# One layer of short convolution and 16-expert mixture: modulation in five groups, and five smaller moves

## Chip, core and metric

One Trainium2 (trn2) chip, one core. The metric is the device time of one execution in microseconds (us). Before the change it is 1913.16 us (median of three runs, 1910.98 to 1913.17). The profile is of one further execution.

## The reference

Everything is float32, with D = 1024 channels and L = 2048 tokens; DEPTH is 1, so the layer is of kind 0 (short convolution).

```python
sh1, sc1, g1, sh2, sc2, g2 = split(silu(c) @ ada_w + ada_b, 6)
hl = rms_norm(x, norm_g[0]) * (1 + sc1) + sh1
b, g, v = split(hl @ sc_w_in, 3)
x1 = x + g1 * ((b * dwconv_centred(g * v, sc_conv)) @ sc_w_out)
h2 = rms_norm(x1, norm_g[1]) * (1 + sc2) + sh2
aff = softmax(h2 @ moe_router)
gate, idx = top_k(aff.T, 256)                     # each of 16 experts picks 256 of 2048 tokens
hid = silu(h2[idx] @ w_gate[e]) * (h2[idx] @ w_up[e])
out = x1 + g2 * scatter_add(gate * (hid @ w_down[e]))
```

## The kernel before

**Precision.** A float32 product is made of three passes: each operand is split into a high part (ACT copies it to fp32r) and a low part (original minus high, by DVE or POOL), and PE adds high*high, high*low and low*high. Weights come in pieces of 512 KB ("raw", loaded on SP's queue), are split into "ws" tiles (8 buffers) and dropped from raw as soon as the low part is made; that releases the next load (`split_high`, `split_low`, `load_to`, lines 199 to 230).

**Stage 1, the in-projection (lines 362 to 625).** The 2048 rows are four quarters of 512. For quarter 0, `load_x` brings four blocks of x, `norm_x` scales each row by its rms (square sum on ACT, power on POOL, product on DVE). Then, for each of 8 k-tiles of 128 channels, `to_hl` turns x by four PE transposes, applies scale A1 and shift sh1 on ACT (twice: high part, and full), and subtracts for the low part. A1 and sh1 are not known at the start: they are columns of `silu(c) @ ada_w`, one pair for each k-tile. `load_ada_cols(k)` brings 1 MB for a k-tile in runs of 128 floats (512 bytes), `ada_cols(k)` adds its 8 row blocks on DVE in two accumulators of 256 columns and then adds the two, `ada_sum(k)` sums over partitions by PE, and `ada_fix(k)` adds bias and gain in three small DVE instructions. The weights of the first two channel tiles (ct 0 and 1; three pieces each, for the three parts of w_in) come in 6 pieces of 128 columns by 1024 rows, the first three in two halves (`load_half`, `split_half`); most of their low parts are made by POOL. The loop at line 544 runs k-tile by k-tile: ct 0 at k, ct 1 with a lag of 3, nine matmuls of 512 columns each (`in_mm`). Behind k = 6 and k = 7 the next quarter's x is normalised and all of its 8 k-tiles are turned. `constants` (line 106) makes tables for the later search, mostly on POOL. Then 30 steps (ps_, ct, q), each 72 matmuls, work off the rest; `in_out` convolves each result and stores it.

**Stage 2, out-projection and router (lines 628 to 940).** 16 blocks of 128 rows.

**Stage 3, experts (lines 943 to 1230).** A short search finds the thresholds of experts 0 and 1; the long one for all 16 (`search_all`, 15 steps, each hit counts on DVE and ACT, a small PE matmul, and an update on DVE) is run in slices: each `tick` runs one slice between matmul groups of experts 0 and 1. `pick_oh(e)` and `pick(e)` turn places into row indices on DVE and PE and gather the expert's rows by two indirect DMAs on POOL. Expert 0's rows are turned by PE (`fetch`), with 6 matmuls on `warm` ahead; the others by a DMA transpose on SP (`turn`) and then put together by DVE and ACT (`join`). `gate_up(e, half)` is 8 k-steps of 24 matmuls of 256 columns, `down(e, half)` 4 steps of 12 matmuls of 512 columns. Both take a function that is called between steps: this is where ticks, picks, turns and joins are placed by hand. The result of an expert is scaled on DVE into `ot` (line 1174) and added into the output by two indirect DMAs of 512 KB on POOL (line 1180).

**Order.** The schedule is manual: each engine works off its instructions in the order in which the program text makes them, and so does each DMA queue (SP's, POOL's). The span ends when the last scatter has landed.

Of the kernel before, what the change touches and what calls it, by code (L numbers as in the profile page):

```python
# [17 lines left out]
P = 128  # L18
# [25 lines left out]
def block_kernel(ctx: ExitStack, tc, x, c, ada_w, ada_b, norm_g, w_in, conv, w_out, router, wg, wu, wd, out):  # L44
# [24 lines left out]
    def row_cols(name, parts):  # L69

        t = consts.tile([P, P], F32, name=name)
        nc.gpsimd.memset(t, 0.0)
        r = 0
        for src, offset, n in parts:
            nc.sync.dma_start(t[r:r + n], dram(src, offset, [[P, n], [1, P]]))
            r += n
        return t, r
# [28 lines left out]
    def constants(scratch):  # L106
# [57 lines left out]
        for t in cnts:  # L164
            nc.vector.tensor_copy(t, zero1)
# [10 lines left out]
    pieces, n_load, n_high, n_done = [], 0, 0, 0  # L176
# [10 lines left out]

    def load_piece(i):
# [7 lines left out]
        nc.sync.dma_start(t, dram(src, offset, ap))  # L196
# [36 lines left out]
    def load_half(i, g):  # L233
        nonlocal n_load
        src, offset, ap, shape = pieces[i]
        if g == 0:
            raws[i] = wpool.tile([P] + shape, F32, name="raw", tag="raw", bufs=n_raw)
            n_load += 1
        n = shape[0] // 2
        nc.sync.dma_start(raws[i][:, g * n:(g + 1) * n],  # L240
                          dram(src, offset + g * n * ap[1][0], [ap[0], [ap[1][0], n], ap[2]]))

    def split_half(i, g, eng=None):
        nonlocal n_high, n_done
        if g == 0:
            ws_of[i] = wpool.tile([P, 2] + pieces[i][3], F32R, name="ws", tag="ws", bufs=n_split)
            n_high += 1
        t, n = ws_of[i], pieces[i][3][0] // 2
        s = slice(g * n, (g + 1) * n)
        nc.scalar.activation(t[:, 0, s], raws[i][:, s], AF.Copy)  # L250
        (eng or nc.vector).tensor_sub(t[:, 1, s], raws[i][:, s], t[:, 0, s].bitcast(F32))
        if g:
            raws.pop(i)
            n_done += 1
            load_to(i + n_raw)

# [105 lines left out]
    with tc.tile_pool(name="mix", bufs=1) as mix:  # L362

        def b4(name):
            return mix.tile([P, D], F32, name=name, tag="b4", bufs=9)
# [21 lines left out]
        def norm_x(q, b, eng=None):  # L387
            t = xq[q][b]
            r = rstd_of(t, junk)
# [5 lines left out]
        def to_hl(q, k, between=lambda: None, eng=None):  # L395
# [127 lines left out]
        for i in range(3):  # L523
            load_half(i, 0)
# [728 lines left out]
```

## Time and profile before

| | |
|---|---|
| median of 3 runs | 1913.16 us |
| the profiled execution | 1912.57 us, of which the span from first to last instruction is 1910.8 us |
| PE busy | 1836.3 us (96%), 11568 matmuls |
| DVE, ACT, POOL busy | 1136.9, 823.7, 304.4 us |
| chain that ended last | PE 89%, DVE 4%, DMA 3% |
| mean granted clock of PE | 0.983 |

PE is busy for nearly all of the span, so time can be had only where PE waits, or where it works at half its clock; the views below look at those stretches: 0 to 87 us, 790 to 837 us, some places up to 960 us, and the last 10 us. Times are from the start of the span.

### The profile page before, as it was taken

The page shows a single profiled execution, that of the slowest core. Times are in us where ns is not written, and L with a number is a line of the kernel's source. Part 1 is how long each engine was busy: PE and PEld are TensorE (multiplying, and loading weights), DVE is VectorE, ACT ScalarE, POOL GpSimd, SP SyncE. Part 2 cuts the span into 40 slices and gives each one's busy share as a digit, 9 for nine tenths or more (in the row PEclk, how much of TensorE's full clock was granted, in tenths as well). Part 3 has the DMA queues.
Part 4 walks back from the last instruction along what each step waited for, and adds up shares of the span by engine and source line. Part 5 has one row for each costly group of instructions (what it writes and reads, how often), then busy time and mean ns, then how long its engine had stood idle before and what let it go on. Part 6 is the DMA issues. An engine that isn't in the chain of part 4 may idle for free.

```text
span 1910.8 us, 29082 instructions
## 1 busy us (share of the span) xinstructions
PE 1836.3 (96%) x11568; PEld 1628.8 (85%) x11568; DVE 1136.9 (60%) x1633; ACT 823.7 (43%) x1046; POOL 304.4 (16%) x457
## 2 busy tenths in 40 slices
PE   4999999999999999579999999999999999999998
PEld 2888888888888888469899999999999999999996
DVE  7654425444325677877766656665765666576653
ACT  3421116211113555547545444554555455445532
POOL 3310002100111122310021102101210211121001
PEclk8999999999999999879999999999999999999999
DMA  9434242344226989466687887779787877878774
GB/s 281 145 113 146 77 160 61 105 137 143 72 72 190 259 257 257 134 219 201 214 249 216 242 248 249 231 227 266 220 239 236 258 219 241 255 238 236 221 231 89
DMA packets 308316, 375.30 MB, mean 196 GB/s; under 512 B 101788, under 2 KB 183764, under 8 KB 308180
## 3 DMA queue, kind: packets, MB, share of 16 engines
q1 hardware_dynamic: 292212, 315.76, 54.3%
q0 software_dynamic: 15968, 57.68, 10.6%
q8 instruction: 91, 1.49, 0.3%
q14 instruction: 45, 0.37, 0.1%
HBM read 300.51 MB, written 50.33 MB: 184 GB/s over the span
## 4 chain that ended last, share of the span: by engine, by line
PE 89%; DVE 4%; DMA 3%; issue 1%; ACT 1%; POOL 1%; SPq 1%; POOLq 0%; DVEq 0%; ACTq 0%
PE pm L1131 12%; PE pm L1133 12%; PE pm L1135 12%; PE pm L451 9%; PE pm L452 9%; PE pm L454 9%; PE pm L1156 6%; PE pm L1154 6%; PE pm L1155 6%; PE pm L656 2%; PE pm L657 2%; PE pm L659 2%; DMA hl<-hl 1%; DMA xt<-in_x_dram 1%; PE pt L398 1%
## 5 line engine op out<-in xcount | busy, mean ns | idle before, releaser
L222 DVE TENSOR_TENSOR ws<-raw,ws 128x1024 fp32r<-128x1024 f32 x434 | 515.6, 1221 | 272.4 <-ACT ws L212 272.4
L212 ACT ACTIVATE ws<-raw 128x1024 fp32r<-128x1024 f32 x437 | 441.3, 1051 | 410.7 <-PE pm L1135 326.9
L1131 PE MATMUL pm<-xT,ws 128*128 128x256 f32 x2048 | 568.8, 278 | 0.0
L1133 PE MATMUL pm<-xT,ws 128*128 128x256 f32 x2048 | 567.1, 277 | 1.0 <-DVE xT L1111 0.9
L1135 PE MATMUL pm<-xT,ws 128*128 128x256 f32 x2048 | 566.8, 277 | 0.0
L1133 PEld LDWEIGHTS pm<-xT,ws 128*128 128x128 f32 x2048 | 385.9, 188 | 2.8 <-DVE xT L1111 1.1
L1131 PEld LDWEIGHTS pm<-xT,ws 128*128 128x128 f32 x2048 | 385.3, 188 | 1.7 <-ACT xT L1110 0.3
L1135 PEld LDWEIGHTS pm<-xT,ws 128*128 128x128 f32 x2048 | 385.2, 188 | 0.0
L451 PE MATMUL pm<-hl,ws 128*128 128x512 f32 x768 | 305.9, 398 | 1.0 <-ACT hl L401 1.0
L452 PE MATMUL pm<-hl,ws 128*128 128x512 f32 x768 | 302.0, 393 | 0.0
L454 PE MATMUL pm<-hl,ws 128*128 128x512 f32 x768 | 217.3, 391 | 0.0
L1180 POOL DMA_INDIRECT out_dram<-ot,idx x32 | 108.0, 3376 | 602.9 <-DVE ot L1174 598.8
L1156 PE MATMUL pm<-ws,hT 128*128 128x512 f32 x512 | 201.6, 394 | 0.0
L1154 PE MATMUL pm<-ws,hT 128*128 128x512 f32 x512 | 201.3, 393 | 0.0
L1155 PE MATMUL pm<-ws,hT 128*128 128x512 f32 x512 | 200.2, 391 | 0.0
L451 PEld LDWEIGHTS pm<-hl,ws 128*128 128x128 f32 x768 | 145.9, 190 | 31.9 <-ACT hl L401 1.4
L452 PEld LDWEIGHTS pm<-hl,ws 128*128 128x128 f32 x768 | 145.9, 190 | 30.5 <-issue 1.0
L454 PEld LDWEIGHTS pm<-hl,ws 128*128 128x128 f32 x768 | 145.5, 189 | 30.8
L461 ACT ACTIVATE cs<-pm 128x512 f32<-128x512 f32 x32 | 19.1, 598 | 332.1 <-issue 261.2
L464 DVE TENSOR_TENSOR u<-cs,pm 128x512 f32<-128x512 f32 x32 | 22.5, 703 | 231.3 <-ACT cs L461 231.3
L1156 PEld LDWEIGHTS pm<-ws,hT 128*128 128x128 f32 x512 | 96.2, 188 | 20.4
L1155 PEld LDWEIGHTS pm<-ws,hT 128*128 128x128 f32 x512 | 96.2, 188 | 20.2
(291 smaller groups left out, 1962.2 us busy)
## 6 DMA issues: line engine op xcount, KB each, us to landing
raw<-in_moe_w_gate_dram SPq DMA_DIRECT2D x128, 512.0 KB, 4.8
raw<-in_moe_w_up_dram SPq DMA_DIRECT2D x128, 512.0 KB, 4.2
raw<-in_moe_w_down_dram SPq DMA_DIRECT2D x128, 512.0 KB, 4.7
raw<-in_sc_w_in_dram SPq DMA_DIRECT2D x45, 512.0 KB, 4.6
xt<-in_x_dram SPq DMA_DIRECT2D x32, 512.0 KB, 7.1
aw<-in_ada_w_dram SPq DMA_DIRECT2D x32, 512.0 KB, 7.1
hl<-in_ada_w_dram SPq DMA_DIRECT2D x32, 256.0 KB, 5.5
hl<-vscr SPq DMA_DIRECT2D x16, 512.0 KB, 4.2
```

Of the source, the lines that this page charges most:

```text
L212: nc.scalar.activation(t[:, 0], raws[n_high], AF.Copy)
L222: (eng or nc.vector).tensor_sub(t[:, 1, ..., s], raw[..., s], t[:, 0, ..., s].bitcast(F32))
L451: nc.tensor.matmul(ps[m], wh, t[:, 0], start=(k == 0), stop=False)
L452: nc.tensor.matmul(ps[m], wl, t[:, 0], start=False, stop=False)
L454: nc.tensor.matmul(ps[m], W(k, m)[0], t[:, 1], start=False, stop=(k == KD - 1))
L1131: nc.tensor.matmul(o, w[:, 0, j, c0], xT[:, 0, k], start=(k == 0 and f % 2 == 0), stop=False, skip_group_check=True)
L1133: nc.tensor.matmul(o, w[:, 0, j, c0], xT[:, 1, k], start=False, stop=False, skip_group_check=True)
L1135: nc.tensor.matmul(o, w[:, 1, j, c0], xT[:, 0, k], start=False, stop=(k == KD - 1), skip_group_check=True)
L1154: nc.tensor.matmul(ps[s], h, w[:, 0, j], start=(k == 0), stop=False)
L1155: nc.tensor.matmul(ps[s], h, w[:, 1, j], start=False, stop=False)
L1156: nc.tensor.matmul(ps[s], l, w[:, 0, j], start=False, stop=(k == KD - 1))
L1180: st = nc.gpsimd.indirect_dma_start(out=out_rows, out_offset=bass.IndirectOffsetOnAxis(ap=idx_of[e][:, s:s + 1], axis=0), in_=ots[s], in_o ...
```

## The change

It does six things. (1) Quarter 0's modulation columns come in five groups, of 1, 1, 2, 2 and 2 k-tiles; groups of two are read in runs of 256 floats (1 KB) and added on DVE in one accumulator of 512 columns. (2) The weights of ct 0 and 1 come together in four steps of 256 rows by 256 columns for each of the three parts, and DVE alone makes their low parts; POOL makes none. `to_hl` is taken apart into `turn_x`, `scale_x` and `low_x`, and quarter 0 is written out with ct 0 and 1 at the same k, with transposes of no use (`wake`) ahead of the first matmul. Five of quarter 1's eight k-tiles are turned within its first step. v_row is loaded on POOL's queue, two of the four row scalings move to ACT, `constants` moves behind the fourth step. (3) The four loads that expert 0's first splits release are issued from POOL's queue, behind the two gathers there; 14, 8 and 3 matmuls of no use stand around its transposes. (4) The search steps of experts 0 and 1 leave out k = 1 and k = 2 behind a stage's begin; the last slice falls behind `down(0, 0)`. (5) Expert 2's turns come one k-step earlier, its joins at k = 7 and at the second step of `down(0, 1)`. (6) The last expert's output goes out in five parts: two left halves behind `down(15, 0)`, then 512, 256 and 256 columns; its last 128 rows are worked off in two lots of 256 columns.

The diff, cut:

```diff
-    def row_cols(name, parts):
+    def row_cols(name, parts, eng=nc.sync):
...
+            eng.dma_start(t[r:r + n], dram(src, offset, [[P, n], [1, P]]))
...
-    pieces, n_load, n_high, n_done = [], 0, 0, 0
+    pieces, n_load, n_high, n_done = [], 6, 6, 6
...
+    load_by = [nc.sync]
...
-        nc.sync.dma_start(t, dram(src, offset, ap))
+        load_by[0].dma_start(t, dram(src, offset, ap))
...
+        if eng:
+            eng.scalar_tensor_tensor(junk, src, 1.0, src, op0=ALU.mult, op1=ALU.mult, accum_out=ss[:, 0:1])
+        else:
+            nc.scalar.activation(junk, src, AF.Square, accum_out=ss[:, 0:1])
...
+        def turn_x(q, k):
+            pt = pt_hl[q, k] = tp.tile([P, QT], F32, name="pt", tag="tp")
             for b in range(4):
                 nc.tensor.transpose(pt[:, b * P:(b + 1) * P], xq[q][b][:, k * P:(k + 1) * P], identf)
...
+        def scale_x(q, k):
+            t = hl[q, k] = hl_tile([P, 2, QT])
             nc.scalar.activation(t[:, 0], pt, AF.Identity, scale=A1[:, k:k + 1], bias=sh1[:, k:k + 1])
             nc.scalar.activation(full, pt, AF.Identity, scale=A1[:, k:k + 1], bias=sh1[:, k:k + 1])
+            return full
+
+        def low_x(q, k, full):
+            nc.vector.tensor_sub(hl[q, k][:, 1], full, hl[q, k][:, 0].bitcast(F32))
+
+        def to_hl(q, k):
+            turn_x(q, k)
+            low_x(q, k, scale_x(q, k))
...
+        groups = [(0, 1), (1, 1), (2, 2), (4, 2), (6, 2)]
+        def load_ada_cols(g):
+            k0, n = groups[g]
+            m = 4 // n
+            ada_t[g] = []
+            for r in range(0, KD, m):
+                t = hl_tile([P, m, 2, n * P], F32)
+                ada_t[g].append(t)
+                for j in range(2):
+                    if n == 1:
+                        nc.sync.dma_start(t[:, :, j], dram(ada_w, r * P * 6 * D + j * D + k0 * P,
+                                                           [[6 * D, P], [6 * D * P, m], [1, P]]))
+                    else:
+                        nc.sync.dma_start(t[:, j], dram(ada_w, (r + j) * P * 6 * D + k0 * P,
+                                                        [[6 * D, P], [D, 2], [1, n * P]]))
...
+        def ada_cols(g, r0=0, r1=KD):
+                ada_a[g] = m2("acc", 2 * n * P)
-                if r < 2:
+                v, t = ada_t[g][r // m][:, r % m].rearrange("p h c -> p (h c)"), ada_a[g]
+                if r == 0:
                     nc.vector.tensor_scalar(t, v, s_col[:, r:r + 1], None, op0=ALU.mult)
                 else:
                     nc.vector.scalar_tensor_tensor(t, v, s_col[:, r:r + 1], t, op0=ALU.mult, op1=ALU.add)
...
+        def ada_sum(g):
...
+        def ada_fix(g, pcol):
+            k0, n = groups[g]
+            s = slice(k0, k0 + n)
+            nc.vector.tensor_add(sh1[:, s], pcol[:, 0], bsh_col[:, s])
+            nc.vector.tensor_add(A1[:, s], pcol[:, 1], bsc_col[:, s])
+            nc.vector.scalar_tensor_tensor(A1[:, s], A1[:, s], 1.0, g0_col[:, s], op0=ALU.add, op1=ALU.mult)
...
         def W_chan(ps_, ct):
+            if ps_ == 0 and ct < 2:
+                return lambda k, m: tuple(w_pair[m, k // 4][:, j, k % 4, ct * P:(ct + 1) * P] for j in range(2))
...
+        def load_w(g):
+            for m in range(3):
+                if g == 0:
+                    w_raw[m, 0] = wpool.tile([P, 4, 2 * P], F32, name="raw", tag="raw", bufs=n_raw)
+                elif g == 2:
+                    w_raw[m, 1] = hl_tile([P, 4, 2 * P], F32) if m else b4("rb", [P, 4, 2 * P])
+                nc.sync.dma_start(w_raw[m, g // 2][:, 2 * (g % 2):2 * (g % 2) + 2],
+                                  dram(w_in, 2 * g * P * 3 * D + m * D, [[3 * D, P], [3 * D * P, 2], [1, 2 * P]]))
...
+        def high_w(g):
+            for m in range(3):
+                if g % 2 == 0:
+                    w_pair[m, g // 2] = wpool.tile([P, 2, 4, 2 * P], F32R, name="ws", tag="ws", bufs=n_split)
+                t, raw, s = part_w(g, m)
+                nc.scalar.activation(t[:, 0, s], raw[:, s], AF.Copy)
...
+        def low_w(g, m):
+            nc.vector.tensor_sub(t[:, 1, s], raw[:, s], t[:, 0, s].bitcast(F32))
...
+        def wake(n):
+            t = mm.tile([P, QT], F32, name="pm", tag="mm")
+            for i in range(n):
+                nc.tensor.transpose(t[:, 0:P], xq[0][0][:, 0:P], identf)
...
+        def mm_pair(i, k):
+            in_mm(pair[i], 0, W_chan(0, i), k)
...
+        load_w(0)
         load_x(0)
+        vrow, nr = row_cols("v_row", [(ada_b, 0, 16), (norm_g, 0, 8), (conv, 0, 24)], nc.gpsimd)
+        for g in range(3):
+            load_ada_cols(g)
+        load_w(1)
+        high_w(0)
+        for m in range(3):
+            low_w(0, m)
+        rs = [rstd_of(xq[0][b], junk) for b in range(4)]
         for b in range(4):
-            norm_x(0, b)
+            norm_x(0, b, nc.scalar if b in (1, 3) else None, rs[b])
         vcols = to_cols("v_col", vrow, nr)
...
+        turn_x(0, 0)
+        wake(14)
+        ada_cols(0)
+        pcol = ada_sum(0)
+        wake(5)
         ada_fix(0, pcol)
+        turn_x(0, 1)
+        full = scale_x(0, 0)
         pair = [new_banks() for _ in range(2)]
+        ada_cols(1, 0, 3)
+        low_x(0, 0, full)
+        ada_cols(1, 3)
+        mm_pair(0, 0)
+        ada_fix(1, ada_sum(1))
+        mm_pair(1, 0)
+        full = scale_x(0, 1)
+        ada_cols(2, 0, 1)
+        low_x(0, 1, full)
+        mm_pair(0, 1)
+        turn_x(0, 2)
+        high_w(1)
+        load_ada_cols(3)
+        load_w(2)
+        ada_cols(2, 1)
+        ada_fix(2, ada_sum(2))
+        for m in range(3):
+            low_w(1, m)
+        load_ada_cols(4)
+        load_w(3)
+        load_x(1)
+        mm_pair(1, 1)
+        turn_x(0, 3)
+        for g in range(2, 5):
+            k = groups[g][0]
+            more_g = g + 1 < len(groups)
+            full = scale_x(0, k)
+            if more_g:
+                ada_cols(g + 1, 0, 2)
+            low_x(0, k, full)
+            mm_pair(0, k)
+            full = scale_x(0, k + 1)
+            if more_g:
+                high_w(g)
+                ada_cols(g + 1, 2, 3)
+            low_x(0, k + 1, full)
+            mm_pair(0, k + 1)
+            if more_g:
+                ada_cols(g + 1, 3)
+                turn_x(0, k + 2)
+            else:
+                rs = [rstd_of(xq[1][b], m2("sq", D, BF), nc.vector) if b % 2 else rstd_of(xq[1][b], junk) for b in range(4)]
                 for b in range(4):
+                    norm_x(1, b, None, rs[b])
                 in_out(pair[0], 0, 0)
+            mm_pair(1, k)
+            if more_g:
+                ada_fix(g + 1, ada_sum(g + 1))
+                for m in range(3):
+                    low_w(g, m)
+            else:
+                to_hl(1, 0)
+            mm_pair(1, k + 1)
+            if more_g:
+                turn_x(0, k + 3)
+        to_hl(1, 1)
+        to_hl(1, 2)
+        load_end[0] = len(pieces)
+        load_to(n_done + n_raw - 1)
...
+            if i == 5:
+                for t in cnts:
+                    nc.vector.tensor_copy(t, zero1.to_broadcast([P, 4]))
...
                 in_mm(ps, q, W_chan(ps_, ct), k)
+                if (ps_, ct, q) == (0, 0, 1) and k + 3 < KD:
+                    to_hl(1, k + 3)
...
+            if i == 3:
+                before, ones_b, tri, slot_r, step, bias, need, zero1, cnts, aux, same, quick = constants(m2)
...
+    def index_parts(parts):
+        for i, (s, c0, n) in enumerate(parts):
+            ix = ix_of[s, c0] = ixs[:, i:i + 1]
+            nc.vector.tensor_scalar(ix, idx_of[E - 1][:, s:s + 1], float(D // n), float(c0 // n), op0=ALU.mult,
+                                    op1=ALU.add)
...
+    def scatter_part(s, c0, n):
+        if parts_of_last:
+            nc.gpsimd.memset(spacer, 0.0)
+        st = nc.gpsimd.indirect_dma_start(
+            out=out.rearrange("b t (c d) -> (b t c) d", d=n), out_offset=bass.IndirectOffsetOnAxis(ap=ix, axis=0),
+            in_=ot_of[E - 1][s][:, c0:c0 + n], in_offset=None, compute_op=ALU.add)
...
+        def finish(s, o, c0, n):
+            nc.vector.scalar_tensor_tensor(ots[s][:, c0:c0 + n], o, gate_of[E - 1][:, s:s + 1], g2b[:, c0:c0 + n],
+                                           op0=ALU.mult, op1=ALU.mult)
+            scatter_part(s, c0, n)
...
+        for k in range(KD):
+            product(0, k)
+        finish(0, ps[0], H, H)
+        for i in range(2):
+            c = slice(i * CAP, (i + 1) * CAP)
+            o = mm.tile([P, CAP], F32, name="pm", tag="mm")
...
+                nc.tensor.matmul(o, h, w[:, 0, j, c], start=(k == 0), stop=False)
+                nc.tensor.matmul(o, h, w[:, 1, j, c], start=False, stop=False)
+                nc.tensor.matmul(o, l, w[:, 0, j, c], start=False, stop=(k == KD - 1))
+            finish(1, o, H + i * CAP, CAP)
...
+            last_down(ps, product)
+            return
...
+        if (e, dh) == (E - 1, 0):
+            index_parts([(0, 0, H), (1, 0, H)])
+            index_parts([(0, H, H), (1, H, CAP), (1, H + CAP, CAP)])
+            for s in range(2):
+                scatter_part(s, 0, H)
...
+    def keep_warm(n):
+        for i in range(n):
+            nc.tensor.matmul(warm, same, ws_of[first][:, 0, 0], start=(i == 0), stop=(i == n - 1))
...
+    keep_warm(14)
+    split_high(first + 4)
+    load_by[0] = nc.gpsimd
     split_to(first + 3)
+    load_by[0] = nc.sync
     for i in (0, 2, 1, 3):
         fetch(0, i, mm)
+        if i > 1:
+            keep_warm(8 if i == 2 else 3)
...
                     (tick(k), turn(1, 0) if k == 7 else None) if k in (2, 4, 5, 6, 7) else None)
             gate_up(0, 1, lambda k: join(1, k // 2 - 2) if k in (4, 6) else
-                    (tick(k), turn(1, 1) if k == 1 else None) if k < 4 else None)
+                    turn(1, 1) if k == 1 else tick(k) if k in (0, 2, 3, 5) else None)
...
-            gate_up(1, 0, lambda k: tick(k) if k else None)
+            gate_up(1, 0, lambda k: tick(k) if k not in (0, 2) else None)
...
-            gate_up(1, 1, lambda k: pick(2) if k == 1 else turn(2, k - 5) if k in (5, 6) else None)
+            gate_up(1, 1, lambda k: pick(2) if k == 1 else turn(2, k - 4) if k in (4, 5) else
+                    join(2, 0) if k == 7 else None)
...
+        down(e - 1, 1, (lambda kk: join(e + 1, 1) if kk == 1 else None) if e + 1 < E else (lambda kk: None))
```

## Rows read from the trace of the kernel before

**Rows 1.** The first stage in one stretch: us, busy us of PE, PEld, DVE, ACT, POOL (instructions), clock, DMA share, GB/s
```profile
0.00:87.00 87.00, 57.12 (x253) 45.40 (x254) 62.29 (x131) 40.93 (x62) 30.23 (x48) 0.90 0.83 234
```
**Rows 2.** What PE waited for, 0 to 130 us: total us, times, longest
```profile
PE pcol L438 <- DVE acc L431: 19.1, 5, 7.0
```
**Rows 3.** DVE (two), POOL (one) by group, 19 to 66 us: busy, mean ns | idle before
```profile
L429 DVE SCALAR_TENSOR_TENSOR acc<-hl,s_col,acc 128x256 f32<-128x256 f32 x42 | 20.7, 550 | 0.1
L431 DVE TENSOR_TENSOR acc<-acc 128x256 f32<-128x256 f32 x7 | 10.5, 1497 | 0.2
...
L222 POOL TENSOR_TENSOR ws<-raw,ws 128x1024 fp32r<-128x1024 f32 x3 | 7.3, 2447 | 9.4 <-ACT ws L212 9.4
```
**Rows 4.** DVE in order of time: start, us, instruction, count
```profile
16.59 0.75 DVE L393 TENSOR_SCALAR xt<-xt,rstd 128x1024 f32<-128x1024 f32 x1 [0.71 <-POOL rstd L283]
...
47.06 0.68 DVE L404 TENSOR_TENSOR hl<-full,hl 128x512 fp32r<-128x512 f32 x1
...
59.79 1.67 DVE L429 SCALAR_TENSOR_TENSOR acc<-hl,s_col,acc 128x256 f32<-128x256 f32 x4
...
75.25 0.75 DVE L469 SCALAR_TENSOR_TENSOR y<-u,v_col,y 128x512 f32<-128x512 f32 x1 [0.85 <-ACT y L468]
76.04 0.75 DVE L471 SCALAR_TENSOR_TENSOR y<-u,v_col,y 128x512 f32<-128x512 f32 x1
...
958.31 2.49 DVE L1053 TENSOR_TENSOR oh<-slot_r,row 128x512 bf16<-128x512 bf16 x4
```
**Rows 5.** Chain that ended last, PE's pieces: start, us
```profile
48.71 0.43 PE pm L452
...
52.44 0.23 PE pm L451
...
59.35 0.50 PE pt L398 x4
```
**Rows 6.** Three stretches, columns as in Rows 1
```profile
45.00:47.00 2.00, 0.46 (x2) 0.01 (x1) 1.97 (x6) 1.45 (x2) 0.00 (x0) 1.00 1.19 291
...
51.00:54.00 3.00, 3.00 (x14) 2.38 (x12) 2.92 (x6) 0.00 (x0) 1.30 (x1) 0.90 1.06 394
...
1907.00:1908.00 1.00, 0.00 (x0) 0.00 (x0) 0.00 (x0) 0.00 (x0) 0.00 (x0) 0.50 1.09 217
```
**Rows 7.** PE in order of time: quarter 1's first matmul, expert 0's start, the last matmul
```profile
86.55 0.39 PE L451 MATMUL pm<-hl,ws 128*128 128x512 f32 x1
...
826.32 1.97 PE L1088 MATMUL pt<-identf,xs 128*128 128x128 f32 x8 [4.10 <-DMA xs<-hscr,idx]
830.77 1.97 PE L1088 MATMUL pt<-identf,xs 128*128 128x128 f32 x8 [2.48 <-DMA xs<-hscr,idx]
832.57 0.58 PE L1131 MATMUL pm<-xT,ws 128*128 128x256 f32 x1
...
1901.56 0.40 PE L1156 MATMUL pm<-ws,hT 128*128 128x512 f32 x1
```
**Rows 8.** POOL in order of time: expert 0's gathers, a scatter of expert 0, the last scatter
```profile
820.70 1.54 POOL L1072 DMA_INDIRECT xs<-hscr,idx  x1 [22.85 <-DVE gate L1077]
822.55 1.80 POOL L1072 DMA_INDIRECT xs<-hscr,idx  x1 [0.30 <-issue]
...
959.73 5.94 POOL L1180 DMA_INDIRECT out_dram<-ot,idx  x1 [0.27 <-issue]
...
1903.02 1.57 POOL L1180 DMA_INDIRECT out_dram<-ot,idx  x1 [3.91 <-DVE ot L1174]
```
**Rows 9.** SP's queue: the first of four loads issued at expert 0's start
```profile
821.29 0.37 SPq L196 DMA_DIRECT2D raw<-in_moe_w_up_dram  x1
```
**Rows 10.** What PE waited for, 130 to 1911 us
```profile
PE pc L965 <- ACT hit L959: 2.5, 2, 1.3
...
PE pm L1133 <- DVE xT L1111: 0.9, 1, 0.9
```

More of the change, by code (lines that the diff above doesn't have):

```diff
@@ L232, in block_kernel @@
     r_of_last = []
[L233 to L255, printed above, removed]
     w_chan = {}
@@ L362, in block_kernel, with b4 @@
     with tc.tile_pool(name="mix", bufs=1) as mix:
[L364 to L365 removed]
+        def b4(name, shape=[P, D]):
+            return mix.tile(shape, F32, name=name, tag="b4", bufs=9)
         def m2(name, n=QT, dt=F32):
@@ L421, in ada_cols @@
+        def ada_cols(g, r0=0, r1=KD):
+            n = groups[g][1]
+            m = 4 // n
             if r0 == 0:
-                ada_a[k] = [m2("acc", 2 * P) for _ in range(2)]
-            acc = ada_a[k]
+                ada_a[g] = m2("acc", 2 * n * P)
             for r in range(r0, r1):
-                v, t = ada_t[k][r // 4][:, r % 4].rearrange("p h c -> p (h c)"), acc[r % 2]
-                if r < 2:
+                v, t = ada_t[g][r // m][:, r % m].rearrange("p h c -> p (h c)"), ada_a[g]
+                if r == 0:
@@ L572, in block_kernel @@
                 for b in range(4):
-                    norm_x(1, b)
-            if k == KD - 1:
+                    norm_x(1, b, None, rs[b])
                 in_out(pair[0], 0, 0)
-            for j in {7: range(2), 8: range(2, 4), 9: range(4, 6), 10: range(6, 8)}.get(k, ()):
-                to_hl(1, j)
-        before, ones_b, tri, slot_r, step, bias, need, zero1, cnts, aux, same, quick = constants(m2)
-        nc.sync.dma_start(rt, dram(router, 0, [[E, P], [E * P, KD], [1, E]]))
-        nc.scalar.activation(rts[:, :, 0], rt, AF.Copy)
@@ L1165, in down @@
         if (e, dh) == (E - 1, 1):
-            for s in range(2):
-                for k in range(KD):
-                    product(s, k)
+            last_down(ps, product)
+            return
         if dh == 0:
@@ L1198, in block_kernel @@
     warm = tp.tile([P, QT], F32, name="warm", tag="tp")
-    for i in range(6):
-        nc.tensor.matmul(warm, same, ws_of[first][:, 0, 0], start=(i == 0), stop=(i == 6 - 1))
+    def keep_warm(n):
[4 more added lines that the diff above has]
+    load_by[0] = nc.gpsimd
     split_to(first + 3)
+    load_by[0] = nc.sync
     for i in (0, 2, 1, 3):
         fetch(0, i, mm)
+        if i > 1:
+            keep_warm(8 if i == 2 else 3)
     for e in range(E):
```

113 lines of the change are left out of this document (30 added, 83 removed).

## The prediction, made blind

> **What bounds the kernel now.** I read the page first: PE is busy 96% of the span, so only places where PE waits or runs at its lower clock can give time. The busy times by stretch say where: in the first 87 us PE is busy 57.12 us [rows 1], and part of that is at half speed, since a matmul of 512 columns takes 0.43 us at 48.71 and 0.23 us at 52.44 [rows 5], which are the 1.2 and 2.4 GHz levels. The waits of PE name the cause: five times, 19.1 us in all, PE waited for the sum of modulation columns on DVE [rows 2]. DVE's groups tell why DVE is late. An accumulation of 256 columns takes 0.42 us undisturbed (four in 1.67 [rows 4]), but 0.55 us in the mean of 42; the closing addition of the same size takes 1.50 us in the mean of seven, while POOL's subtraction takes 2.45 us [rows 3]. DVE loses some 42 x 0.13 + 7 x 1.08 = 13 us to POOL's subtractions. So the stage is bound by DVE, and PE, fed in drops, loses its clock: from 45 to 47 us PE worked 0.46 of 2 us and the granted clock was still 1.00, at 48.71 the pitch is the lower one, and after unbroken work it is the upper one at 52.44 [rows 5, 6]. Quarter 1's first matmul is at 86.55 [rows 7]. After that I read three short places: expert 0's start, where the second gather lets PE go on at 830.77 only [rows 7]; the search, 2.5 us in two waits, and one wait of 0.9 us for a join [rows 10]; and the end, where the span runs on 8.8 us behind the last matmul (1910.8 - 1901.96 [rows 7]).
>
> **1. First stage.** Removed: all of POOL's subtractions there, the seven closing additions, half of the accumulations' instruction count for six k-tiles. Added on DVE: twelve low parts of weights and the low parts of x that POOL made, 0.68 us each [rows 4]. An addition of 512 columns onto itself is not in this stage; the nearest rows are the two chained ones at 75.25 and 76.04, 0.79 us apart [rows 4]; its bounds are 0.70 (only the width grows) and 0.84 (twice the 0.42). I take 0.79, and 0.50 for a chained one of 256.
>
> *Start.* x's fourth block is scaled by 17.3 us now [rows 4], behind 1.05 MB of columns; afterwards it is behind 0.79 MB of weights and two scalings are on ACT, so 16.5. The first group's columns are now behind x: 1.05 MB at 291 GB/s [rows 6] are 3.6 us more. With 8 chained additions they are summed at about 19.3, fixed at 20.6, and the first matmul comes at 21.4.
>
> *DVE's list from 20.6:* 8 additions of group 1 (4.0), a low part of x (0.7), sum and fix (1.2), 8 additions of group 2 (6.3), a low part (0.7), a wait for ACT's scaling (0.8): the third sum at 34.3. Each further group is sum and fix 1.2, three weight low parts 2.0, two of x 1.4, 8 additions 6.3 = 10.9: sums at 45.2 and 56.1. PE's work in a group is 36 x 0.23 + two sets of transposes of 0.5 [rows 5] + the sum 0.6 = 9.9, so DVE leads by little.
>
> *End.* Behind 56.1 PE has the sum 0.6, five nine-matmul lots of 2.07, and five sets of transposes of 0.5, two of them quarter 1's late ones: 13.4 with small waits. Quarter 1's first matmul is at 69.5; five sets of its transposes are still to come inside the step (2.5), so 72.0 stands against 86.55: 14.5. PE still has gaps before the third sum, where the clock can fall; I take 0.5 off for that (0 to 4). **14.0 us gained**, 9 to 18.
>
> *What is hidden.* The loads: 12.9 MB up to the last group's columns, from 2.3 us at 291 to 394 GB/s [rows 6] (runs of 512 bytes and of 4 KB; runs of 1 KB lie between), end by 46.7 at the latest, and DVE wants those rows from 52. v_row's three loads on POOL's queue have until the first fix. `constants` lies behind four steps of 16.5 us on POOL, which has only small work there. The six double weight tiles keep 6 of 8 split buffers until the second step, so ACT waits with the third next piece until the middle of that step; it is wanted at the step's end, 8 us later.
>
> **2. Expert 0's start.** Four loads of 512 KB go out on SP's queue from 821.29, between the two gathers at 820.70 and 822.55 [rows 8, 9], and share the DMA engines with them: the first takes 5.6 us to PE's transposes, the second 8.2 (830.77 [rows 7]). On POOL's queue the loads stand behind both gathers. Bounds for the second: 5.6 (828.2) to 8.2 (no gain). I take 5.6, as it then moves alone. Eight warming matmuls (1.8) end at about the same time, so the first matmul comes 1.8 behind 828.4, at 830.2 for 832.57: 2.4. If the warming holds the clock, a stretch like 48.71 to 52.44 at the lower level is saved, half of 3.7 us: 1.8. Together **4.0**, 0 to 6. The moved loads are wanted only at the fifth k-step, 11 us later.
>
> Here a row and a rule differ. POOL's own gathers took 1.54 and 1.80 us [rows 8] while DVE ran the subtractions of the first splits, and a scatter beside DVE's list for expert 3 took 5.94 instead of 1.57 [rows 4, 8]. So one kind of DVE work holds POOL's issue and the other doesn't; behind 824.4 DVE has neither, and I charge nothing. The Trainium skill (SBUF — State Buffer, "SBUF: two separate sides") speaks against such a move: a DMA issued from POOL has its descriptors written by POOL's cores, which certain DVE instructions lock out, and it advises SP's or ACT's queue. By that rule, with each load held as the 5.94 us scatter was, the time is that of rival C.
>
> **3. Search and expert 2.** The two waits of 2.5 us [rows 10] stand at slices that follow each other directly behind an expert's activation work on ACT and DVE; with a k-step of 2.7 us (24 matmuls of 0.114) left out they go. One slice too few is left, so the last one falls behind `down(0, 0)` and expert 2's list is later: 0 to one step of `down` (12 x 0.23 = 2.8); the list is nearly on time now, I take 0.8. Net **1.7**, -0.3 to 2.5. The join's wait of 0.9 [rows 10] goes, since the second join is a step earlier; but the first join at k = 7 may hold DVE and ACT until the second turn frees its buffer. Net **0.4**, -1.5 to 0.9.
>
> **4. The end.** Today 512 KB follow the last scaling. Afterwards 128 KB do: at 217 GB/s [rows 6] 2.4 us become 0.6. The scaling of 256 columns is 0.3 shorter, and the transfer's slow beginning and end shrink a little: **2.4**. The matmuls cost the same (48 of half the width). POOL issues five scatters; with 1.57 us each [rows 8] the fourth is issued before the last scaling ends. Held like the one of 5.94 they would cost 4: -2 to 3.
>
> **Sum.** 14.0 + 4.0 + 1.7 + 0.4 + 2.4 = 22.5 us off the profiled execution's 1912.57: 1890.1. The median of the runs is 0.6 above that execution, so **1890.5 us**.
>
> **Rivals.**
> A. *PE stays at the lower level all through the first stage* (slower). For it: the row pair of 45 us and 48.71, where a gap of under 2 us was enough. Then a nine-matmul lot is 3.84 us; from the third sum at 34.4 there are 13 lots (50), 8 sets of transposes of 0.6 and two sums (1.2): quarter 1 begins at 91, counts as 94, 7.5 later than now. The same gate takes the 1.8 at expert 0, so the other parts keep 6.7, and the clock's rise inside quarter 1 costs 1.8 more: 1912.6 + 7.5 + 1.8 - 6.7 = 1915. It decides from quarter 1's first matmul at 91 on. Against it: at half speed PE has no gaps left (15.4 us of matmuls in a DVE group of 10.9), and with no gap it rose at 52.44. The Trainium skill (TensorE: Matmul & The Clock Gate, "HAM oscillation — how this bites in real kernels") describes a kernel in which the gate falls again in every wait for data, group by group; that is this rival. 5%.
> B. *The loads bind.* If runs of 1 KB in pairs of rows move at 230 GB/s, the last columns land at 59.8 and are summed at 63.8 instead of 56.1: 7.7 less, 1898. From under 266 GB/s it decides. Against: 291 with runs half as long [rows 6]. 17%.
> C. *POOL's issue is held at expert 0.* Four loads of 5.94 us end at 848; the seventh k-step wants them at 846.5, and the next expert's gather stands behind them: the 4.0 is lost, 1894.5. 10%.
> The change does what it says in part 2 only if the loads are what delays the second gather; otherwise 1892.5, inside my own case.
>
> **Numbers.** My case 68%, A 5%, B 17%, C 10%. Its own bounds (additions 0.70 to 0.84, the clock, the gather, the joins) make it 1883 to 1897. The range reaches to B and C: 1882 to 1900. About 0.2% (3.8 us) is what a measurement of this kernel tells from no change. All cases but A are faster by more; A lies at its edge. Faster 0.93, same 0.04, slower 0.03.
>
> **What the profile will show.** Right: quarter 1's first matmul (a transposes set between its lots) at 67 to 72; DVE's 512-column additions at 0.79 apart, no POOL subtraction before it; expert 0's first matmul 2 to 3 us behind the second gather at the upper pitch of 0.11; no `pc` wait over 0.5 us; some 6.5 us from the last matmul to the end. Wrong: 0.43 us matmuls beyond 40 us (A); DVE waiting for hl's loads beyond 40 us (B); POOL's loads at 5 us each (C).

## The result and the profile after

The changed kernel takes **1901.51 us** (median of five runs, 1901.02 to 1901.69) against 1913.0 before (median of five): ratio 0.9942, with a 95% interval of 0.9929 to 0.9956. Forecast were 1890.5 and a range of 1882 to 1900. The direction was right; of the 22.5 us forecast, 11.5 came.

The profiled execution has a span of 1899.5 us (1910.8 before), so 11.3 us are to be found in two traces. The starts of the same work in both, from the timelines:

| start of | before | changed | ahead by |
|---|---|---|---|
| last modulation sum of quarter 0 on PE | 63.78 | 56.14 | 7.64 |
| last nine matmuls of quarter 0 | 81.31 | 69.95 | 11.36 |
| quarter 1's first matmul | 84.41 | 75.47 | 8.94 |
| first matmul behind quarter 1's eight lots | 100.83 | 94.30 | 6.53 |
| first gather of expert 0 | 820.70 | 815.26 | 5.44 |
| expert 0's first matmul | 832.57 | 824.61 | 7.96 |
| `pick(1)`'s first matmul | 843.31 | 833.45 | 9.86 |
| expert 2's second half of `gate_up` | 988.79 | 979.76 | 9.03 |
| last matmul | 1901.56 | 1892.60 | 8.96 |
| end | 1910.8 | 1899.5 | 11.3 |

Read down, the first stage gave 6.5 (14.0 forecast), the start of expert 0 4.4 (4.0), the search and expert 2 took 0.8 (2.1 to be gained), and the end gave 2.3 (2.4). Another 1.1 went between quarter 1 and the first gather, where the change moves little but `constants`.

The modulation sums, which made PE wait 19.1 us before [rows 2], are nearly gone. What PE waited for from 0 to 130 us in the changed kernel:

```profile
PE pt L379 <- DVE xt L372: 7.1, 4, 3.9
...
PE pcol L436 <- DVE acc L426: 3.6, 2, 2.0
```

The first line is new: PE waits for normalized rows of x, 3.9 us of it once at the start, and three times for quarter 1. This is the end of the stage on PE in order of time:

```profile
56.14 0.95 PE L436 MATMUL pcol<-ones_f,acc 128*128 128x1 f32 x8
...
64.99 0.85 PE L454 MATMUL pm<-hl,ws 128*128 128x512 f32 x3
65.68 0.27 PE L379 MATMUL pt<-identf,xt 128*128 128x128 f32 x1
66.89 0.33 PE L379 MATMUL pt<-identf,xt 128*128 128x128 f32 x1 [0.94 <-DVE xt L372]
68.35 0.33 PE L379 MATMUL pt<-identf,xt 128*128 128x128 f32 x1 [1.14 <-DVE xt L372]
69.82 0.48 PE L379 MATMUL pt<-identf,xt 128*128 128x128 f32 x1 [1.14 <-DVE xt L372]
69.95 0.77 PE L451 MATMUL pm<-hl,ws 128*128 128x512 f32 x1
...
72.65 1.48 PE L454 MATMUL pm<-hl,ws 128*128 128x512 f32 x3
73.93 1.78 PE L379 MATMUL pt<-identf,xt 128*128 128x128 f32 x8
75.47 0.48 PE L451 MATMUL pm<-hl,ws 128*128 128x512 f32 x1
```

Up to 65.68 PE has hardly a gap. Then four transposes, 0.5 us of work, take until 69.95, each behind one scaled block of quarter 1. The lot of nine matmuls behind them, the last of quarter 0, had all it needs by 65.7 and stands in PE's queue (e2 runs it there). When its turn comes the clock has fallen: 69.95 to 73.93 is 4.0 us for what takes 2.04 at the upper level. The granted clock, last column but two, shows it (columns as in [rows 1]):

```profile
65.00:70.00 5.00, 1.78 (x9) 0.97 (x7) 2.86 (x5) 0.00 (x0) 3.70 (x7) 0.86 0.61 227
70.00:75.00 5.00, 5.00 (x16) 4.02 (x16) 3.22 (x6) 2.06 (x3) 1.03 (x3) 0.50 0.01 3
```

What the blocks wait for is on DVE and POOL, in order of time:

```profile
61.81 1.22 DVE L257 SCALAR_TENSOR_TENSOR sq<-xt 128x1024 bf16<-128x1024 f32 x1
...
64.61 0.75 DVE L372 TENSOR_SCALAR xt<-xt,rstd 128x1024 f32<-128x1024 f32 x1 [0.43 <-POOL rstd L262]
66.08 0.75 DVE L372 TENSOR_SCALAR xt<-xt,rstd 128x1024 f32<-128x1024 f32 x1 [0.71 <-POOL rstd L262]
...
64.66 0.75 POOL L260 TENSOR_SCALAR ss<-ss 128x1 f32<-128x1 f32 x1
65.50 0.55 POOL L262 TENSOR_TENSOR rstd<-ss,mhalf 128x1 f32<-128x1 f32 x1
66.13 0.75 POOL L260 TENSOR_SCALAR ss<-ss 128x1 f32<-128x1 f32 x1
```

A block is scaled every 1.47 us, in turns: DVE waits for POOL's root, and POOL's small operation on one column begins with DVE's scaling and ends with it, 0.75 us. Before, the same norms stood at `k == 6`, with two more lots of quarter 0 in PE's queue ahead of the first transposes, and more between the next ones.

### The profile page after: what moved, and what is told of

It reads as the page before. It is cut to its first block, busy times and chain, and to the rows that moved or that the text cites. A ratio compares the mean times of both kernels' runs of the same rounds, so it can differ in the third digit from the quotient of the medians.

```text
span 1899.5 us, 29186 instructions
## 1 busy us (share of the span) xinstructions
PE 1839.6 (97%) x11630; PEld 1631.4 (86%) x11630; DVE 1128.3 (59%) x1614; ACT 824.2 (43%) x1047; POOL 296.3 (16%) x459
## 4 chain that ended last, share of the span: by engine, by line
PE 89%; DVE 4%; issue 2%; DMA 2%; ACT 2%; POOL 1%; SPq 0%; POOLq 0%; DVEq 0%; ACTq 0%
PE pm L1198 12%; PE pm L1200 12%; PE pm L1202 12%; PE pm L454 8%; PE pm L451 8%; PE pm L452 8%; PE pm L1267 6%; PE pm L1265 6%; PE pm L1266 6%; PE pm L723 3%; PE pm L726 3%; PE pm L724 3%; DVE ws L222 1%; DMA tr<-xs 1%; PE pt L379 1%
## 5 line engine op out<-in xcount | busy, mean ns | idle before, releaser
L1267 PE MATMUL pm<-ws,hT 128*128 128x512 f32 x504 | 198.4, 394 | 0.0
L1265 PE MATMUL pm<-ws,hT 128*128 128x512 f32 x504 | 198.2, 393 | 0.0
L1266 PE MATMUL pm<-ws,hT 128*128 128x512 f32 x504 | 197.1, 391 | 0.0
L454 PEld LDWEIGHTS pm<-hl,ws 128*128 128x128 f32 x768 | 144.8, 189 | 31.6 <-DVE hl L389 1.2
L461 ACT ACTIVATE cs<-pm 128x512 f32<-128x512 f32 x32 | 19.1, 598 | 317.4 <-issue 234.9
```

The lines of the kernel that those rows point to most:

```text
L454: nc.tensor.matmul(ps[m], W(k, m)[0], t[:, 1], start=False, stop=(k == KD - 1))
L1265: nc.tensor.matmul(ps[s], h, w[:, 0, j], start=(k == 0), stop=False)
L1266: nc.tensor.matmul(ps[s], h, w[:, 1, j], start=False, stop=False)
L1267: nc.tensor.matmul(ps[s], l, w[:, 0, j], start=False, stop=(k == KD - 1))
```

## Experiments

Two theories stood at first. **N**: quarter 1's norms hold PE, and the lower clock follows from that wait. **O**: only PE's order is at fault. Each is an edit of the changed kernel, and its time is read against the kernel before on the same chip.

### e1: the norms one group earlier

```diff
             mm_pair(0, k + 1)
+            if g == 3:
+                rs = [rstd_of(xq[1][b], junk) for b in range(4)]
...
-                rs = [rstd_of(xq[1][b], m2("sq", D, BF), nc.vector) if b % 2 else rstd_of(xq[1][b], junk) for b in range(4)]
```

> Edit: the four sums of squares of quarter 1's rows (all on ACT) and POOL's roots come one group earlier, while ACT waits for the last group's sums; only the four scalings stay behind quarter 0's last low part, and DVE makes no squares. Theory N (the norms of quarter 1 hold PE: its 4.2 us from 65.7 to 69.95 and the lower clock behind it): the last scaling ends by 65.2 instead of 69.8, PE's four transposes follow each other at 65.7, the last nine-matmul lot of quarter 0 takes 2.1 us instead of 3.98, quarter 1's first matmul comes at 69.5 to 70.5 instead of 75.47, and the time falls by 5 to 6 us, to 1895.5 to 1896.5. Rival O (only PE's order is at fault: a ready lot stands behind transposes, the norms would be covered): the wait moves, 0 to 2 us, 1899.5 to 1901.5.

1896.85 us (1894.08 to 1897.92), ratio 0.9914 [0.9900, 0.9927]. In its timeline:

```profile
64.49 2.73 DVE L372 TENSOR_SCALAR xt<-xt,rstd 128x1024 f32<-128x1024 f32 x4
...
68.37 0.60 PE L379 MATMUL pt<-identf,xt 128*128 128x128 f32 x4
68.72 0.48 PE L451 MATMUL pm<-hl,ws 128*128 128x512 f32 x1
...
71.68 0.48 PE L451 MATMUL pm<-hl,ws 128*128 128x512 f32 x1
```

The four blocks are scaled in one go, PE waits for none, and the last lot takes 2.2 us (68.72 to 70.89). Quarter 1 begins at 71.68, 3.8 us earlier, although the last modulation sum came later here (58.81). N holds and O falls. That it isn't 70 is the clock again, in the wait ahead of the third sum (e8). Counted from the last sum, so without what came ahead of it, quarter 1 follows after 12.9 us here and in the three other executions with these early norms (e7, e8, e12), and after 18.3 to 19.4 in the seven that keep the changed kernel's norms and PE's order around them. The edit does two things at once, squares and roots earlier and none of the squares on DVE; which of them gives how much is not separated.

### e2: PE's order alone

```diff
-            else:
-                to_hl(1, 0)
             mm_pair(1, k + 1)
...
+        to_hl(1, 0)
         to_hl(1, 1)
```

> Edit: only PE's order; quarter 1's first transposes go behind quarter 0's last lot of nine matmuls. Rival O: PE has no wait left of over 0.5 us, quarter 1's first matmul by 71, 4 to 6 us gained, 1895.5 to 1897.5. Theory N: the lot runs at 65.7 at the upper pitch and ends at 67.8, but the last scaled block still comes at 69.8, so the transposes and the first low part are where they were (about 74) and quarter 1's first matmul comes at 74 to 75.5; 0 to 1.5 us gained, 1900 to 1901.5.

1901.58 us, ratio 0.9944 [0.9930, 0.9957]: nothing gained. PE now works through that lot at the upper level, and then waits:

```profile
68.93 0.38 PE L379 MATMUL pt<-identf,xt 128*128 128x128 f32 x2
69.56 0.33 PE L379 MATMUL pt<-identf,xt 128*128 128x128 f32 x1 [0.25 <-DVE xt L372]
71.03 0.77 PE L379 MATMUL pt<-identf,xt 128*128 128x128 f32 x5 [1.14 <-DVE xt L372]
73.77 1.12 PE L379 MATMUL pt<-identf,xt 128*128 128x128 f32 x4 [1.98 <-ACT full L385]
74.54 0.78 PE L451 MATMUL pm<-hl,ws 128*128 128x512 f32 x1
```

Quarter 1 begins at 74.54 (74 to 75.5 were expected under N), at the lower level. The wait had moved behind the lot.

### e3: the scalings on ACT

```diff
-                    norm_x(1, b, None, rs[b])
+                    norm_x(1, b, nc.scalar, rs[b])
```

> Edit: quarter 1's four scalings of 128 x 1024 on ACT instead of DVE, squares and roots as they are. Theory L (a DVE operation on fp32 holds POOL, so each small POOL operation lasts as long as DVE's scaling beside it): POOL's first small operation of each block falls from 0.75 us to 0.2 to 0.35, and the chain per block from 1.47 us to ACT's own 1.05 to 1.15; the last scaling ends 1 to 1.5 us earlier, 1900 to 1900.5. Rival: POOL's operation is slow by itself there; it stays at 0.75 and the chain gets longer by 0.3 per block, 1902.5.

1898.61 us, ratio 0.9931 [0.9916, 0.9946], more than theory L asked for. POOL, in order of time:

```profile
61.54 0.79 POOL L260 TENSOR_SCALAR ss<-ss 128x1 f32<-128x1 f32 x1 [46.55 <-ACT junk L259]
...
63.91 0.19 POOL L260 TENSOR_SCALAR ss<-ss 128x1 f32<-128x1 f32 x1
64.19 0.55 POOL L262 TENSOR_TENSOR rstd<-ss,mhalf 128x1 f32<-128x1 f32 x1
```

Without DVE's scaling beside it the small operation takes 0.19 instead of 0.75 us; the first one still runs beside DVE's squares. So L holds, and quarter 1 begins at 72.60, 17.2 us behind the last sum (55.36) instead of 18.3 to 19.4: the turns between the two engines cost 1.1 to 2.1 of the 5.4 to 6.5 that e1 gives. The Trainium skill (SBUF — State Buffer, "SBUF: two separate sides") says that certain DVE operations and POOL's share one pair of ports by an exclusive lock, held for a whole instruction: the trace agrees, 0.75 against 0.19.

### e4: the search and expert 2 as before

```diff
-                    turn(1, 1) if k == 1 else tick(k) if k in (0, 2, 3, 5) else None)
+                    (tick(k), turn(1, 1) if k == 1 else None) if k < 4 else None)
...
-            gate_up(1, 0, lambda k: tick(k) if k not in (0, 2) else None)
+            gate_up(1, 0, lambda k: tick(k) if k else None)
...
-            gate_up(1, 1, lambda k: pick(2) if k == 1 else turn(2, k - 4) if k in (4, 5) else
-                    join(2, 0) if k == 7 else None)
+            gate_up(1, 1, lambda k: pick(2) if k == 1 else turn(2, k - 5) if k in (5, 6) else None)
...
+            down(e - 1, 1, lambda kk: join(2, kk - 1) if kk in (1, 2) else None)
...
```

> Edit: search slices, and expert 2's turns and joins, as in the kernel before. Theory S (the new order of slices and joins costs more than it gives: from the matmuls of pick(1) to expert 2's first matmul 113.0 us against 111.3 before): two waits of 1.2 to 1.3 us for the search come back, the wait of 1.3 for the second join and the four of 0.3 for the one-hots go, 1.5 to 2 us faster, 1899.5 to 1900. Rival (the forecast: the new order is worth 2.1): 1903 to 1904.

1899.96 us, ratio 0.9938 [0.9924, 0.9951], which can't be told from the changed kernel. The time lies in the range of theory S, but S falls too, with its rival: by the traces, the two orders cost the same. What PE waited for between `pick(1)` and expert 2, first in the changed kernel (840 to 950 us):

```profile
PE pm L1200 <- DVE xT L1178: 1.8, 2, 0.9
PE pi L1128 <- DVE oh L1120: 1.4, 4, 0.3
PE pm L1198 <- ACT xT L1177: 1.3, 1, 1.3
PE pT L335 <- DVE tbits L283: 0.4, 1, 0.4
PE pc L1032 <- ACT hit L1026: 0.4, 1, 0.4
```

and in e4 (833 to 978 us):

```profile
PE pc L1032 <- ACT hit L1026: 2.5, 2, 1.3
PE pm L1200 <- DVE xT L1178: 0.9, 1, 0.9
PE pcount L1065 <- DVE ge L1059: 0.5, 1, 0.5
PE pi L1128 <- DVE oh L1120: 0.3, 1, 0.3
```

The 2.5 us of the search do go in the new order, and come back elsewhere: 0.9 for a join of expert 1 (at 871.59; the other 0.9 is there before as well [rows 10]), 1.4 instead of 0.3 for expert 2's one-hots, which DVE begins later since one slice falls behind `down(0, 0)`, and 0.4 for a slice: 2.4 in all (`pT`'s 0.4 stands for `pcount`'s 0.5). The 1.3 for ACT's part of a join is in this one execution only. From `pick(1)`'s matmul to expert 2's second half, nine executions with the new order took 144.4 to 146.3 us, mean 145.2, and five with the old 144.8 to 146.0, mean 145.5. Part 3 is worth 0.3 us at most: four of these five, and only one of the nine, have the longer pitch told at the end, 0.8 us that no wait shows.

### e5 and e6: the two halves of expert 0's start

```diff
-    load_by[0] = nc.gpsimd
```

> Edit: expert 0's four weight loads go back to SP's queue, between the gathers; the warming matmuls stay. Theory G (the loads delay the second gather): from the first gather's issue to the end of the second set's transposes as before, about 2.3 us later than in the changed kernel, first matmul of expert 0 some 11.7 us behind the first gather's issue instead of 9.35; if PE's longer wait lowers the clock, 1.9 more; 1903.5 to 1905.5. Rival W (the warming matmuls did it, the queue is nothing): within 0.5 of the changed kernel.

1903.73 us, ratio 0.9958 [0.9944, 0.9972], as G has it; but the first matmul came 14.52 us behind the first gather's issue, later than G's 11.7: the second gather's rows came 11.48 behind it, against 10.07 before, and the transposes and three warming matmuls behind them ran at a clock of 0.50 to 0.70.

```diff
-    keep_warm(14)
+    keep_warm(6)
...
-            keep_warm(8 if i == 2 else 3)
+            pass
```

> Edit: six warming matmuls instead of 14 ahead of the first gather's transposes, and none behind them; the loads stay on POOL's queue. Theory W: granted clock 0.5 at expert 0's first matmuls as in the kernel before, 17 matmuls at 0.21 instead of 0.114 us and both sets of transposes 0.5 to 1 us longer, so pick(1)'s first matmul 1.9 to 3 us later against the first gather; 1903.4 to 1904.5. Rival G (the queue alone did it): the clock rises by itself, 0 to 0.5.

1902.99 us, ratio 0.9943 [0.9928, 0.9959]. By the time alone the warming gives nothing that can be told (0.9942 for the changed kernel). The traces tell more: from the first gather's issue to `pick(1)`'s matmul it is 22.61 us before, 18.19 in the changed kernel (833.45 - 815.26), 23.19 in e5, and 20.04 in e6. The eleven executions with both halves took 18.1 to 18.7. The changed kernel:

```profile
815.26 1.55 POOL L1139 DMA_INDIRECT xs<-hscr,idx  x1 [22.88 <-DVE gate L1144]
817.10 1.79 POOL L1139 DMA_INDIRECT xs<-hscr,idx  x1 [0.30 <-DVE ws L222]
818.90 0.81 POOL L196 DMA_DIRECT2D raw<-in_moe_w_up_dram  x1
...
822.97 1.09 PE L1155 MATMUL pt<-identf,xs 128*128 128x128 f32 x8
823.82 0.96 PE L1317 MATMUL warm<-ws,same 128*128 128x512 f32 x3
824.61 0.28 PE L1198 MATMUL pm<-xT,ws 128*128 128x256 f32 x1
```

e5, with the loads between the gathers on SP's queue:

```profile
820.00 1.09 PE L1155 MATMUL pt<-identf,xs 128*128 128x128 f32 x8 [0.82 <-DMA xs<-hscr,idx]
...
825.83 1.97 PE L1155 MATMUL pt<-identf,xs 128*128 128x128 f32 x8 [2.85 <-DMA xs<-hscr,idx]
```

e6, without the warming:

```profile
826.70 0.58 PE L1198 MATMUL pm<-xT,ws 128*128 128x256 f32 x1
...
829.09 0.41 PE L1202 MATMUL pm<-xT,ws 128*128 128x256 f32 x1
```

Both theories hold in the traces, and the halves need each other: the loads on POOL's queue save 4.5 to 5.1 us while the warming is there, the warming 1.3 to 2.0 with the loads there (one trace of either); the warming alone (e5 against before) gives nothing, since a wait of 2.85 us remains and the transposes behind it take 1.97 instead of 1.09 us.

### e7 and e8: the early norms with the old search, and a filled wait

e7 has the edits of e1 and e4. e8 adds transposes that PE repeats, into the same place, ahead of the second and third sums:

```diff
...
         mm_pair(0, 0)
+        turn_again(0, 1, 6)
         ada_fix(1, ada_sum(1))
...
+        turn_again(0, 2, 16)
         ada_fix(2, ada_sum(2))
...
```

> Edits of e1_norms_early and e4_search_old together. If the two are independent: quarter 1's first matmul near 71 and, from pick(1) to expert 2's first matmul, 110.2 us; 1895 to 1897. If the old order of the search only looked better by the scatter between executions, as e1 again: 1896.5 to 1897.

> As e7_best, and PE repeats transposes that it has just made (6 ahead of the second sum, 16 ahead of the third), into the same place, while it waits for DVE's sums. Theory K (the clock falls in these waits, and the lots behind them at 0.43 us a matmul delay DVE's next low part and so the next sums): every matmul of 512 columns from 27 us on at 0.23, the last sum at 56 or earlier, 1 to 2.5 us below e7_best. Rival D (DVE alone sets the pace up to the last sum): the same time as e7_best within 0.5.

e7: 1895.14 us (1894.18 to 1899.42), ratio 0.9912 [0.9897, 0.9926]; quarter 1 begins at 69.74. The old order of the search adds nothing to e1: from `pick(1)` to expert 2's first matmul e7 took 110.6 us, e1 110.3. e8: 1897.32, ratio 0.9922 [0.9908, 0.9935]; quarter 1 begins at 68.67. The stretch from 35 to 40 us shows what the third sum's wait does to the clock (columns as before, the last but two is the clock). e8:

```profile
35.00:40.00 5.00, 4.88 (x28) 3.86 (x27) 4.03 (x10) 2.95 (x5) 0.00 (x0) 1.00 1.10 350
```

and e1, where PE had come to that sum early and waited 3.6 us for it:

```profile
35.05 1.44 PE L436 MATMUL pcol<-ones_f,acc 128*128 128x1 f32 x8 [3.60 <-DVE acc L426]
...
35.00:40.00 5.00, 4.95 (x17) 4.21 (x18) 3.41 (x9) 1.45 (x2) 0.00 (x0) 0.55 1.10 349
```

At the lower level PE does 17 instructions instead of 28 there, DVE's next low part waits for PE's transposes, and the last sum comes at 58.81 (e1) against 55.81 (e8). So K holds for the stage, by 1.1 us against e7. In the whole time it can't be seen, e8's median is even 2.2 above e7's: between quarter 1 and the first gather e8 lost 3.4 us, e7 1.5.

### e9: no transposes to wake PE

```diff
-        wake(14)
...
-        wake(5)
```

> Edit: the 19 transposes that only keep PE at work ahead of its first matmul (14 and 5) are left out. Theory A' (rival A in part: the early clock sets the stage): quarter 0's first three lots at 0.43 us a matmul, the second sum's matmul later by 1 us or more and the last sum (56.1 in the changed kernel, 55.8 to 57.3 in the runs that do not touch it) at 58 or later; 1 to 4 us slower. Theory D (DVE's list and the loads set the pace up to the third sum, PE waits for both sums anyway): the first three lots at 0.43, PE's waits of 1.6 and 2.0 to 3.6 shrink by what the lots grow, the last sum at 55.5 to 57.5, the time within 1 us of the changed kernel.

1901.49 us, ratio 0.9946 [0.9930, 0.9963]: no difference that can be measured. The first lot ran at 0.43 us a matmul, and the second sum was no later for it (26.07, against 26.34 in the changed kernel), as D has it. But then PE came to the third sum early, waited 3.6 us, and the clock was 0.50 from 35 to 40 us; so the last sum at 58.27 is where A' put it, though by another wait, and quarter 1 began at 77.66, 2.2 us later than in the changed kernel. Without e8's filling the clock falls behind the one wait or the other, in e4 and e7 behind both (0.66 from 25 to 30 us, 0.67 and 0.68 from 35 to 40).

### e10 to e12: the same chip, and the end

> No edit: the changed kernel once more, beside the other two. If the 1.1 us that its profiled execution lost between quarter 1 and the first gather, and the 1.3 us of one wait for a join of expert 2, belong to the change, they come again: 232.1 us from the out-projection's first matmul to the first gather with 2.0 us ahead of it, and 146.3 us from pick(1)'s matmul to expert 2's second half. If they are scatter between executions, one or both are elsewhere (1.1 to 2 ahead of it, 231.9 to 235; 144.7 to 145.6), the time 1900 to 1902.5.

1900.59 us, ratio 0.9939 [0.9925, 0.9952]. The wait of 1.3 for the join is not there, so it was scatter. The loss of about 1 us ahead of the first gather came again (0.9), but e2, e4 and e5, which edit nothing there either, lost 0.1 to 0.2, and e8 3.4. Over the thirteen executions it lies between -0.1 and 3.4, and in the four with early norms between 1.5 and 3.4: part of what these gain may go again there, and no run settles it.

e11 puts back the two scatters of whole rows:

```diff
-            last_down(ps, product)
-            return
+            for s in range(2):
+                for k in range(KD):
+                    product(s, k)
...
-            for s in range(2):
-                scatter_part(s, 0, H)
...
```

> Edit: the last expert's output goes out in two scatters of whole rows, as before. The fourth step of the forecast (128 KB instead of 512 KB behind the last scaling): span end 9.2 us behind the last matmul's start instead of 6.9, 2.0 to 2.6 us slower than e10_changed_again. Rival (the slow end of any transfer sets it, the size is nothing): within 0.5.

1904.16 us, ratio 0.9962 [0.9949, 0.9976]. Its span ends 9.55 us behind its last matmul (1899.9 - 1890.35), that of e10 7.04 behind its own. The fourth step holds, at 2.5; the medians lie 3.6 apart, with a wider scatter of e11's runs (1901.86 to 1907.13).

> No edit against e7_best: on one chip with the changed kernel. If the early norms are worth 4 to 6 us there too, 1895 to 1897 where e10_changed_again has 1900 to 1902.5; if the distance came from comparing different chips, within 2 us of it.

1896.49 us, ratio 0.9917 [0.9904, 0.9931]: on one chip the kernel of e7 is 4.1 us below the changed kernel, with four of its five runs (1893.37 to 1900.12) below all five of the other. So the distance is not one between chips. e1, which keeps the new search, does as well within what can be told (0.9914, on another chip).

## Why the prediction was wrong, step by step

**1, first stage: the start and DVE's list right, the end wrong.** First matmul forecast at 21.4, came at 22.37; the sums were forecast at 34.3, 45.2 and 56.1, and PE took them at 35.18, 45.68 and 56.14. The additions cost 0.78 in a chain (seven in 5.47) for 0.79. The step that failed is "Behind 56.1 PE has the sum 0.6, five nine-matmul lots of 2.07, and five sets of transposes of 0.5 ...: 13.4 with small waits". The work is nearly as written (four sets of transposes stand there, not five, and three of them are quarter 1's; where the norms are early, all of it takes 12.9), but the waits are not small: quarter 1 began at 75.47 instead of 69.5. Of these 6.0, some 3.8 are the norms (four transposes from 65.68 to 69.95 for 0.5 of work), 1.9 the lot at the lower level and 0.7 the transposes behind it, less 0.5 for the set too many. I listed what hides the loads, `v_row` and `constants`, but the diff also moves quarter 1's norms from `k == 6` to behind the last low part, with two squares more on DVE and POOL's eight small operations in turn with DVE's scalings. I did not cost that move at all, and its cover was gone. e1 gives back what it took (12.9 us from the last sum to quarter 1 instead of 19.3).

The same step had a second error, in reading: the matmul at 86.55 [rows 7] begins quarter 1's second lot, not its first. The first stands at

```profile
84.41 0.48 PE L451 MATMUL pm<-hl,ws 128*128 128x512 f32 x1
```

of the kernel before, straight behind its last eight transposes. That is 2.1 us of gain which was never there. With 2.1 and 6.0 off, 14.5 is 6.4; the table has 6.53. (Quarter 1's late transposes cost 2.4 for 2.5 forecast.)

**2, expert 0: right.** First matmul 9.35 us behind the first gather's issue against 11.87: 2.5 for 2.4; the clock another 1.9 for 1.8. The four loads on POOL took 0.75 to 0.81 us each, so nothing of DVE's held them, and rival C falls. The lockout shows in the operations of quarter 1's norms instead.

**3, search and expert 2: wrong by 2 us.** That the two waits go was right; what failed is taking all of them for a gain, with 0.8 charged for expert 2's later list. What came in their place cost 0.9 for expert 1's join, which I did not have at all, 1.1 for the one-hots and 0.4 for a slice. The join's wait of 0.9, forecast to go, stayed. A slice that makes PE wait less brings PE sooner to the next thing that DVE owes.

**4, the end: right**, 2.3 in the first pair of traces and 2.5 in e11, for 2.4. (Its last 0.3, for the transfer's slow beginning and end, was taken from no row, and no run shows it by itself.)

In the first pair of traces the span fell by 11.3 us for 22.5: 7.5 of the 11.2 that are missing are step 1's, 2.9 step 3's, 1.1 went between quarter 1 and the first gather, and step 2 gave 0.4 more than forecast.

**Rivals.** A fell as put: PE was at the upper level for most of the stage, and beyond 40 us its sign, matmuls at 0.43, showed only in the last lot. Its mechanism, the clock lost in a wait for DVE, was real and took 1.9 us at the last lot and, in some executions, more at the third sum. B fell: DVE waited for no load behind 40 us, and the runs of 1 KB moved at 348 to 352 GB/s from 20 to 40 us. The range missed by 1.5 us since no case of mine held a wait between the last sum and quarter 1; all of them priced what the diff adds to the stage, none what it moves to the stage's end.

## What to carry to other kernels

When a stage is made faster, list everything that the old schedule did under its cover, and ask of each where it now stands; work moved to behind the last step of the stage was paid in full here (3.8 us), and once more by the lower clock behind the wait (1.9). Count a stage's end in matmuls, not by a shape in the timeline, and look for the matched instruction in both kernels. A wait that is taken away on the path counts only for the distance to the next one.

## What the runs showed of the hardware

**The clock can fall behind short waits, and not always behind the same ones.** In executions of kernels that are alike there, the same stretch may run at either level. It can also fall where PE hardly waited: in e3's out-projection PE did 8 transposes and 16 matmuls of 16 columns from 585.7 to 588.8, with one wait of 0.25 us, and then matmuls of 512 columns without a gap:

```profile
589.00:591.00 2.00, 2.00 (x8) 1.59 (x8) 1.31 (x2) 0.00 (x0) 0.56 (x1) 0.76 1.14 351
591.00:593.00 2.00, 2.00 (x6) 1.55 (x5) 0.00 (x0) 0.00 (x0) 0.00 (x0) 0.50 1.01 330
593.00:595.00 2.00, 2.00 (x9) 1.59 (x8) 0.00 (x0) 0.00 (x0) 0.00 (x0) 0.88 1.08 393
```

That cost some 1.7 us (an estimate: 2 us times what the clock lacks to 1 in each row). In the changed kernel's trace the same work, with the same wait, is followed by a clock of 1.00 (591 to 599 us). Such dips are part of the scatter of 1 to 3 us between executions here, and effects of 1 us were therefore read from traces and not from times.

**Two engines in turn on small operations.** POOL's operation on one column, 0.19 us alone, takes as long as DVE's fp32 scaling beside it, 0.75. The chain that changes between the two engines paid that at each turn: 1.47 us a block, against 1.04 with the scalings on ACT (four in 4.26).

**A longer pitch at full clock, not explained.** The first half of expert 2 took 23.86 us in four of five executions with the old order of the search, and 23.03 in the changed kernel, with a wait of 0.9 us in either; in the kernel before the pitch of its matmuls (start to start) is 0.118 us all through, in the changed kernel 0.113, both at a granted clock of 1.00. The order does not decide it alone: e8, with the old one, has 0.113, and e6, with the new one, 0.118. The cause stays open.
